# Moving four weight sums from even to odd channel tiles in the gate and up stage of a two-layer block

## The chip, the core and the metric

The kernel runs on one core of a Trainium2 chip. The metric is the device time of one execution in microseconds (us), given as a median of several runs. The engines are PE (matrix products), DVE (elementwise work and PSUM reads), ACT (activations and copies), POOL (elementwise work on SBUF) and SP, which here only issues DMA transfers. Each engine takes its instructions in a fixed order and waits at the first one whose inputs, or whose output buffer, are not ready.

## What is computed

The reference is a mixer block with a mixture of experts, then an attention block, then a feed-forward layer on 1024 tokens of width 1024. Only the last layer matters here:

```
h = rms_norm_2(x, norm_ffn)
gu = h @ w_gate_up                                   # (1024, 1024) @ (1024, 5632)
x = x + (silu(gu[:, :2816]) * gu[:, 2816:]) @ w_down # (1024, 2816) @ (2816, 1024)
```

## The kernel before, in words

`phase6` computes this layer. Both products are done as 2x2 block products with seven multiplications in place of eight (products 1 to 7), each in full precision from a high and a low part of every operand, so that one product is 4 x 3 = 12 matmuls of 128x128 by 512.

**Gate and up.** The 2816 hidden channels make 22 tiles of 128 (`FF`), j = 0 to 21. `seq` lists the products: tiles 0 and 1 mixed, then tile by tile in the order 1, 4, 6, 7, 5, 2, 3 for j = 2 to 19, then 20 and 21 mixed. The main loop (from L2258 on) does four things at step i. It calls `prep(i + 5)`, which turns the weights of the product five steps ahead into a high part on ACT (L1942) and a low part on DVE (L1943). It calls `product(i)` on PE (L1958). It calls `evac(i - 1)`, which reads the finished product from PSUM (DVE L1978 to L1997, ACT L1974, L1994 and L1998) and, where all is there, multiplies gate by up on POOL (`act0` L2001, `act1` L2004). At some steps it adds side work on POOL. The loop is written out by hand for PE, DVE, ACT and POOL: each of these runs the instructions in the order of the code. SP's order is chosen by the scheduler when the program is built.

**Side work.** `load(j)` fetches the weights of a tile, and `sums(j)` forms four sums of them on POOL (L1926 to L1929) for products 5, 6, 7 and 3, just before the first `prep` of tile j. When an odd tile's last product has been read, at the first step of the next even tile, `pair_sums` forms four sums of the activations of the last two tiles on DVE (L2037 to L2040), in buffers called l12 and l34, and `keep` (L2032) stores them to DRAM (`fd`) for the down projection. `right_load(i)` and `right_sums(i)` fetch two blocks of the down projection's weights, form four sums of them on POOL (L2058 to L2061), in buffers r12 and r34, and store them to DRAM (`td`). There are 11 such i. Before the change i = 1 to 9 go to the even tiles 2 to 18, i = 0 to tile 9 and i = 10 to tile 15.

**Buffers.** All of these live in slots of 4 KB per partition, taken from the front of a queue (`get`) and given back at its end (`put`). `put` is a matter of the order of the code only; the engine that first writes the new tenant waits until the last reader of the old one, a store to DRAM too, is done. So a different order of `get` and `put` gives every later buffer another slot, and other waits.

**Down projection.** After the loop the same scheme runs over the stored activations and sums. It reads `fd`, `td` and the weights back.

The mark of a tile that is used below is the start of `act1` (L2004) on POOL, once a tile, or the DVE instruction that leads to it (L1997).

Of the kernel before, what the change touches and what calls it, by code (L numbers as in the profile page):

```python
# [49 lines left out]
class _K:  # L50
# [1819 lines left out]
    FF = 22  # L1870
# [3 lines left out]
    def phase6(self):  # L1874
        nc, I = self.nc, self.I
        V, G, A = nc.vector, nc.gpsimd, nc.scalar
        FF, H = self.FF, 512
# [4 lines left out]
        FP = FF // 2  # L1882
# [10 lines left out]
        def get(key, shape=(P, 1024), dt=F32):  # L1893
            held[key] = free.popleft()
            return self.S(held[key], shape, dt)

        def put(*keys):
            for k in keys:
                free.append(held.pop(k))
# [18 lines left out]
        def load(j):  # L1918
            for n, c in (("g", 0), ("u", FF)):
                st[j][n] = get((n, j), (P, KC, P))  # L1920
                nc.sync.dma_start(st[j][n], w[:, :, (c + j) * P:(c + j + 1) * P])
# [13 lines left out]
        def prep(i):  # L1935
            prepped.append(i)
            j, p = seq[i]
            if "done" not in st[j]:
                sums(j)
            src = st[j][self.PAIRS[p][0]]  # L1940
            t = get(("w", i), (P, 2, 4, P), F32R)
            A.activation(t[:, 0], src, AF.Copy)  # L1942
            V.tensor_sub(t[:, 1], src, t[:, 0])  # L1943
            st[j]["w", p] = t
            d = st[j]["done"]
            d.add(p)
            for k, n in (("g", {1, 2}), ("u", {4}), ("s12", {5, 6}), ("s34", {7, 3})):
                if n <= d and p in n:
                    put((k, j))

        def product(i):
            j, p = seq[i]
            tag, ps = st[j]["b", p] = bank()
            t = st[j].pop(("w", p))
            xs = X[self.PAIRS[p][1]]
            for k in range(4):
                for n, (a, b) in enumerate(((0, 0), (0, 1), (1, 0))):
                    nc.tensor.matmul(ps, t[:, a, k], xs[k][:, b], start=(k == 0 and n == 0), stop=(k == 3 and n == 2))  # L1958
            put(("w", i))
# [70 lines left out]
        def keep(i, o, src, dst=fd):  # L2030
            n = src.shape[-1]
            nc.sync.dma_start(dst[i * P:(i + 1) * P, o * H:o * H + n], src)  # L2032
# [17 lines left out]
        def right_load(i):  # L2050
            for n in range(2):
                right[i, n] = get(("r", i, n))
                nc.sync.dma_start(right[i, n], wd[:, 2 * i + n, :])

        def right_sums(i):
            a, b = right.pop((i, 0)), right.pop((i, 1))
            t12, t34 = get(("r12", i), (P, 2, H)), get(("r34", i), (P, 2, H))
            G.tensor_sub(t12[:, 0], a[:, H:], a[:, 0:H])  # L2058
            G.tensor_sub(t12[:, 1], b[:, H:], t12[:, 0])
            G.tensor_sub(t34[:, 0], b[:, H:], a[:, H:])  # L2060
            G.tensor_sub(t34[:, 1], b[:, 0:H], t12[:, 1])  # L2061
            keep(i, 0, t12.rearrange("p a b -> p (a b)"), td)
            keep(i, 2, t34.rearrange("p a b -> p (a b)"), td)
            put(*((n, i) for n in ("r12", "r34")), *(("r", i, n) for n in range(2)))
# [103 lines left out]
        def pump(now, spare, most=2, splits=1):  # L2168
            n = 0
            while (coming and coming[0][0] + LAG <= now and need[coming[0][1][:2]] <= now + AHEAD  # L2170
                   and n < splits and len(free) > spare):
                op_split()
                n += 1
            n = 0
            while ops and n < most and (loads[0] % 2 or (len(free) > spare + KEEP and len(raw) < RAWS)):
                op_load(now)
                n += 1
# [6 lines left out]
        def x_load():  # L2184
            for t in xs[:2]:
                x[t] = get(("x", t))
                nc.sync.dma_start(x[t], self.h2d[t * P:(t + 1) * P, :])
            del xs[:2]

        with self.tc.manual_schedule(engines={E.PE, E.DVE, E.Activation, E.Pool}):  # L2190
# [67 lines left out]
            for i in range(6, len(seq)):  # L2258
                j = seq[min(i + LEAD + 7, len(seq) - 1)][0]
                if "g" not in st[j]:  # L2260
                    load(j)
                while i + LEAD >= len(prepped) and len(prepped) < len(seq):
                    prep(len(prepped))
                product(i)
                evac(i - 1)
                j, p = seq[i]
                if 2 <= j < FF - 2 and (j % 2 == 0 or j in (9, 15)):
                    m = j // 2 if j % 2 == 0 else {9: 0, 15: FP - 1}[j]
                    if p == 1:
                        right_load(m)  # L2270
                    if p == 4:
                        right_sums(m)
                if i + 1 == len(seq) or seq[i][0] == FF - 1:
                    put(*((self.PAIRS[p][1], k) for k in range(4)))
                if i >= len(seq) - 14:
                    if i >= len(seq) - XL:
                        x_load()
                    pump(4 * (i - len(seq)), 6 if i < len(seq) - 8 else 12 - SP * (8 - len(xs)), 4, 4)
# [123 lines left out]
```

## Time and profile before

| what | value |
|---|---|
| time, median of 3 runs | 2239.24 us (2236.61 to 2244.52) |
| time of the profiled execution | 2236.43 us |
| its span, first to last instruction | 2234.6 us |
| what lies around the span | 1.8 us |
| PE busy over the span | 91% |
| DVE, ACT, POOL busy over the span | 67%, 40%, 40% |
| gate and up, the tiles that go one by one (j = 2 to 19) | 1573 to 1942 us |

A row of the timeline gives the start of a group of instructions, its length, engine, line of the program, operation and operands, how many instructions it merges, and in brackets how long the engine had been idle before it and what ended that. A row of the chain of waits gives start, length and what was being waited for.

### The profile page before, as it was taken

To read this page: it belongs to the slowest core of one execution; us is meant where nothing else is said; L and a number is where in the kernel's file an instruction comes from. 1 tells how busy PE (TensorE), PEld (TensorE's weight loads), DVE (VectorE), ACT (ScalarE), POOL (GpSimd) and SP (SyncE) were. 2 spreads that over 40 slices of the span, in tenths; PEclk is the share of its full clock that TensorE was granted. 3 is DMA by queue.
4 is the path that set the end of the run, shared out by engine and by line. 5 is a ranking of instruction groups with operands and counts; after the bars stand their busy time and mean duration, and the time that the engine had idled before them with its cause. 6 is when DMAs were issued, how large, how long until landed. Compare 5 with 4: busy or idle time off the path is not lost.

```text
span 2234.6 us, 30292 instructions
## 1 busy us (share of the span) xinstructions
PE 2031.7 (91%) x10594; PEld 1499.3 (67%) x10594; DVE 1496.2 (67%) x2264; ACT 901.4 (40%) x1589; POOL 902.2 (40%) x655
## 2 busy tenths in 40 slices
PE   4988999998899998999868998999999899989995
PEld 2677888887455654666527874687878787767774
DVE  6687886526454534767426349637877777699998
ACT  2544447412244423645305149534222222244443
POOL 2365352331111121222112027305656666567786
PEclk9999999899699999999979999999999999999998
DMA  7352110416799899999984310321454454575541
GB/s 266 123 187 78 38 29 29 134 41 245 294 384 350 310 332 392 355 385 373 381 319 145 119 38 2 133 95 55 153 170 156 163 171 148 184 264 167 193 151 76
DMA packets 204739, 426.09 MB, mean 191 GB/s; under 512 B 18580, under 2 KB 99202, under 8 KB 204578
## 3 DMA queue, kind: packets, MB, share of 16 engines
q1 hardware_dynamic: 195218, 402.62, 49.9%
q0 software_dynamic: 9360, 21.46, 4.1%
q8 instruction: 85, 1.39, 0.3%
q14 instruction: 76, 0.62, 0.1%
HBM read 361.36 MB, written 65.01 MB: 191 GB/s over the span
## 4 chain that ended last, share of the span: by engine, by line
PE 41%; DMA 21%; DVE 18%; issue 10%; POOL 5%; ACT 3%; SPq 1%; POOLq 0%; DVEq 0%; ACTq 0%
DMA s<-w 9%; PE a L282 7%; PE a L270 4%; PE a L812 4%; DMA x2d<-s,dstp 3%; DVE s L1943 2%; PE t L2326 2%; PE a L2326 2%; DMA s<-w_ada 2%; DMA s<-ffn_w_gate_up 2%; DMA x2d<-s,dsti 2%; PE a L1412 2%; DVE s L2161 2%; DVE s L509 1%; PE r L2326 1%
## 5 line engine op out<-in xcount | busy, mean ns | idle before, releaser
L1344 DVE TENSOR_TENSOR s<-s,s 128x1024 fp32r<-128x1024 f32 x168 | 206.2, 1240 | 122.1 <-ACT s L1343 117.3
L282 PE MATMUL a<-s,s 128*128 128x512 f32 x1008 | 244.6, 400 | 9.9 <-ACT s L503 9.9
L1343 ACT ACTIVATE s<-s 128x1024 fp32r<-128x1024 f32 x168 | 175.8, 1057 | 152.8 <-PE t L1403 74.5
L282 PEld LDWEIGHTS a<-s,s 128*128 128x128 f32 x1008 | 190.4, 191 | 52.3 <-ACT s L503 10.2
L1943 DVE TENSOR_TENSOR s<-s,s 128x512 fp32r<-128x512 f32 x154 | 162.9, 1074 | 73.6 <-ACT s L1942 73.6
L1958 PE MATMUL a<-s,s 128*128 128x512 f32 x708 | 173.5, 395 | 1.2 <-ACT s L1942 1.0
L1958 PE MATMUL t<-s,s 128*128 128x512 f32 x648 | 161.4, 404 | 13.1 <-DVE s L1943 9.6
L1354 POOL DMA_INDIRECT s<-h2d,toki x38 | 42.9, 1129 | 312.1 <-PE r L1370 148.7
L1958 PEld LDWEIGHTS a<-s,s 128*128 128x128 f32 x708 | 133.6, 189 | 33.5 <-ACT s L1942 1.9
L1942 ACT ACTIVATE s<-s 128x512 fp32r<-128x512 f32 x154 | 91.1, 622 | 159.6 <-DVE s L1943 71.7
L1958 PEld LDWEIGHTS t<-s,s 128*128 128x128 f32 x648 | 124.4, 193 | 44.9 <-DVE s L1943 11.3
L2161 DVE TENSOR_TENSOR s<-s,s 128x512 fp32r<-128x512 f32 x129 | 139.0, 1114 | 0.0
L1403 PE MATMUL t<-s,s 128*128 128x512 f32 x384 | 119.5, 407 | 5.3 <-DVE s L1487 3.1
L1958 PE MATMUL r<-s,s 128*128 128x512 f32 x492 | 120.2, 394 | 0.3
L1403 PE MATMUL a<-s,s 128*128 128x512 f32 x336 | 106.5, 413 | 7.0 <-DVE s L1372 3.5
L270 PE MATMUL a<-s,s 128*128 128x512 f32 x432 | 107.1, 399 | 2.7 <-DVE s L1602 2.7
L1958 PEld LDWEIGHTS r<-s,s 128*128 128x128 f32 x492 | 92.2, 188 | 22.3 <-DVE s L1943 1.1
L2160 ACT ACTIVATE s<-s 128x512 fp32r<-128x512 f32 x154 | 84.7, 621 | 41.4 <-POOL s L2161 18.1
L2326 PE MATMUL a<-s,s 128*128 128x512 f32 x348 | 94.7, 396 | 4.6 <-DVE s L2347 1.7
L2326 PE MATMUL t<-s,s 128*128 128x512 f32 x348 | 90.8, 399 | 8.0 <-DVE hraw L2338 2.5
L1412 PE MATMUL a<-s,s 128*32 128x256 f32 (+1 forms) x736 | 89.5, 464 | 8.1 <-ACT s L1386 3.3
L812 PE MATMUL a<-s,s 128*128 128x512 f32 x384 | 92.7, 397 | 0.6 <-DVE s L666 0.6
(576 smaller groups left out, 4374.3 us busy)
## 6 DMA issues: line engine op xcount, KB each, us to landing
s<-w SPq DMA_DIRECT2D x384, 512.0 KB
s<-w_ada SPq DMA_DIRECT2D x48, 512.0 KB
s<-ffn_w_gate_up SPq DMA_DIRECT2D x44, 512.0 KB
s<-fd SPq DMA_DIRECT2D x77, 256.0 KB
fd<-s SPq DMA_DIRECT2D x33, 512.0 KB
h2d<-s SPq DMA_DIRECT2D x24, 512.0 KB
s<-w_in SPq DMA_DIRECT2D x22, 512.0 KB
s<-ffn_w_down SPq DMA_DIRECT2D x22, 512.0 KB
```

Of the source, the lines that this page charges most:

```text
L270: nc.tensor.matmul(ps[:m], a[:, k, :], b(k, h), start=(k == 0 and n == 0), stop=(k == KC - 1 and n == 2))
L282: nc.tensor.matmul(ps[h][:m], a[:, k, :], b(k, h), start=(k == 0 and n == 0), stop=(k == KC - 1 and n == 2))
L812: nc.tensor.matmul(ps, a.of(k, t), W[k][:, b], start=(k == 0 and n == 0), stop=(k == 7 and n == 2))
L1343: nc.scalar.activation(hi, raw, AF.Copy)
L1344: V.tensor_sub(lo, raw, hi)
L1403: nc.tensor.matmul(pp[h], a[:, k // 4, s], w[:, h * 512:(h + 1) * 512], start=(k == 0 and n == 0), stop=(k == 7 and n == 2))
L1412: nc.tensor.matmul(p_[M * g:M * g + M, 0:N], x[:, k_, :], w[:, :, g, :], start=(k_ == 0), stop=(k_ == 7))
L1942: A.activation(t[:, 0], src, AF.Copy)
L1943: V.tensor_sub(t[:, 1], src, t[:, 0])
L1958: nc.tensor.matmul(ps, t[:, a, k], xs[k][:, b], start=(k == 0 and n == 0), stop=(k == 3 and n == 2))
L2161: (G if loads[1] % SHARE == SHARE - 1 else V).tensor_sub(u[:, 1], t, u[:, 0])
L2326: nc.tensor.matmul(ps[p], a[:, e, q * P:(q + 1) * P], b[:, f], start=(i == g[0] and n == 0), stop=(i == g[-1] and n == 2))
```

## The change

Nothing is added or taken away: the same 11 loads, 44 sums and 22 stores are called at other steps. The sums i = 1 to 9 go from tile 2i to tile 2i + 1, at the same two steps of the tile (load with product 1, sums with product 4). The sums i = 0 and i = 10 go from tiles 9 and 15 to tiles 8 and 14, and there to later steps: load with product 7, sums with product 2.

```diff
-                if 2 <= j < FF - 2 and (j % 2 == 0 or j in (9, 15)):
-                    m = j // 2 if j % 2 == 0 else {9: 0, 15: FP - 1}[j]
+
+                if 2 < j < FF - 2 and j % 2:
                     if p == 1:
-                        right_load(m)
+                        right_load(j // 2)
                     if p == 4:
-                        right_sums(m)
+                        right_sums(j // 2)
+                if j in (8, 14):
+                    if p == 7:
+                        right_load({8: 0, 14: FP - 1}[j])
+                    if p == 2:
+                        right_sums({8: 0, 14: FP - 1}[j])
```

In the rows below a buffer is written as slot and number: s8_18032 is the tenant 18032 of slot 8. POOL from `act1` of tile 9 to `act1` of tile 10, and up to the sums after it, before:

```order
L2004 TENSOR_TENSOR s8_17937<-s8_17937,hraw_17918 128x512
L2058 TENSOR_TENSOR s44_18026<-s7_18004 128x512
L2059 TENSOR_TENSOR s44_18026<-s13_18006,s44_18026 128x512
L2060 TENSOR_TENSOR s34_18027<-s13_18006,s7_18004 128x512
L2061 TENSOR_TENSOR s34_18027<-s13_18006,s44_18026 128x512
L1926 TENSOR_TENSOR s8_18038<-s23_17878 128x512
L1927 TENSOR_TENSOR s8_18038<-s8_18038,s43_17876 128x512
L1928 TENSOR_TENSOR s5_18039<-s43_17876,s23_17878 128x512
L1929 TENSOR_TENSOR s5_18039<-s43_17876,s8_18038 128x512
L2001 TENSOR_TENSOR s34_18095<-s34_18095,m_18024 128x512
L2004 TENSOR_TENSOR s34_18095<-s34_18095,hraw_18076 128x512
L1926 TENSOR_TENSOR s20_18176<-s16_18036 128x512
```

The same place now:

```order
L2004 TENSOR_TENSOR s29_17937<-s29_17937,hraw_17918 128x512
L1926 TENSOR_TENSOR s13_18026<-s43_17878 128x512
L1927 TENSOR_TENSOR s13_18026<-s13_18026,s16_17876 128x512
L1928 TENSOR_TENSOR s33_18027<-s16_17876,s43_17878 128x512
L1929 TENSOR_TENSOR s33_18027<-s16_17876,s13_18026 128x512
L2001 TENSOR_TENSOR s5_18083<-s5_18083,m_18020 128x512
L2004 TENSOR_TENSOR s5_18083<-s5_18083,hraw_18064 128x512
L2058 TENSOR_TENSOR s22_18164<-s43_18142 128x512
L2059 TENSOR_TENSOR s22_18164<-s6_18144,s22_18164 128x512
L2060 TENSOR_TENSOR s13_18165<-s6_18144,s43_18142 128x512
L2061 TENSOR_TENSOR s13_18165<-s6_18144,s22_18164 128x512
L1926 TENSOR_TENSOR s8_18176<-s31_18024 128x512
```

In the even tile 10 the next tile's four sums now follow `act1` at once, and in the odd tile 11 the four down sums stand between `act1` and the next tile's sums.

SP at the start of tile 10 now stores the activations of tile 9 and then l12 and l34:

```order
L2032 DMA fd_15856<-s29_17937 128x1024
L2032 DMA fd_15856<-s8_17996 128x1024
L2032 DMA fd_15856<-s23_17997 128x1024
L1921 DMA s38_18172<-ffn_w_gate_up_2 128x8x128
L2053 DMA s43_18142<-ffn_w_down_2 128x1024
```

l12 is in slot 8 and l34 in slot 23. ACT in tile 10, from the conversion for product 3 on, before:

```order
L1942 ACTIVATE s31_18008<-s22_17881 128x512
L1974 ACTIVATE m_18024<-r1_17979 128x512
L1942 ACTIVATE s22_18044<-s43_17876 128x512
L1942 ACTIVATE s27_18060<-s23_17878 128x512
L1942 ACTIVATE s44_18078<-s8_18038 128x512
```

and now, there and then at the same place of tile 11:

```order
L1942 ACTIVATE s38_18004<-s27_17881 128x512
L1974 ACTIVATE m_18020<-r1_17979 128x512
L1942 ACTIVATE s8_18032<-s16_17876 128x512
L1942 ACTIVATE s23_18048<-s43_17878 128x512
L1942 ACTIVATE s29_18066<-s13_18026 128x512
...
L1974 ACTIVATE m_18162<-a1_18125 128x512
L1942 ACTIVATE s23_18182<-s20_18022 128x512
L1942 ACTIVATE s22_18198<-s31_18024 128x512
L1942 ACTIVATE s13_18216<-s8_18176 128x512
```

In the even tile the two conversions behind `u1` (L1974) now write the slots of l12 and l34; in the odd tile the second and third write the slots of r12 and r34 (22 and 13), which the POOL rows above fill in the same tile.

## Rows read from the trace of the kernel before

**Rows 1.** The page: span, and busy time of the engines.
```profile
span 2234.6 us, 30292 instructions
```

**Rows 2.** Waits of PE from 1555 to 1960 us: total, times, longest.
```profile
PE t L1958 <- DVE s L1943: 9.6, 3, 5.6
```

**Rows 3.** Timeline of PE: start, length, engine, line, what, count, idle before.
```profile
1744.84 4.63 PE L1958 MATMUL t<-s,s 128*128 128x512 f32 x10 [5.63 <-DVE s L1943]
...
1774.56 2.93 PE L1958 MATMUL r<-s,s 128*128 128x512 f32 x12
...
1813.36 2.94 PE L1958 MATMUL r<-s,s 128*128 128x512 f32 x12
```

**Rows 4.** Timeline of POOL: `act1` of tiles 1, 8 to 11, 14, 15, 17, two sums.
```profile
1573.12 1.29 POOL L2004 TENSOR_TENSOR s<-s,hraw 128x512 f32<-128x512 f32 x1 [0.18 <-ACT hraw L1998]
...
1714.56 1.29 POOL L2004 TENSOR_TENSOR s<-s,hraw 128x512 f32<-128x512 f32 x1 [1.89 <-ACT hraw L1998]
1715.80 1.77 POOL L2058 TENSOR_TENSOR s<-s 128x512 f32<-128x512 f32 x1
...
1726.01 1.29 POOL L1929 TENSOR_TENSOR s<-s,s 128x512 f32<-128x512 f32 x1
...
1736.09 1.30 POOL L2004 TENSOR_TENSOR s<-s,hraw 128x512 f32<-128x512 f32 x1 [1.89 <-ACT hraw L1998]
...
1759.96 1.30 POOL L2004 TENSOR_TENSOR s<-s,hraw 128x512 f32<-128x512 f32 x1 [1.89 <-ACT hraw L1998]
...
1775.16 1.29 POOL L2004 TENSOR_TENSOR s<-s,hraw 128x512 f32<-128x512 f32 x1 [1.89 <-ACT hraw L1998]
...
1838.15 1.30 POOL L2004 TENSOR_TENSOR s<-s,hraw 128x512 f32<-128x512 f32 x1 [1.89 <-ACT hraw L1998]
...
1858.36 1.30 POOL L2004 TENSOR_TENSOR s<-s,hraw 128x512 f32<-128x512 f32 x1 [1.89 <-ACT hraw L1998]
...
1897.14 1.29 POOL L2004 TENSOR_TENSOR s<-s,hraw 128x512 f32<-128x512 f32 x1 [1.89 <-ACT hraw L1998]
```

**Rows 5.** Timeline of DVE: the even tile 12, from L1997 to L1997.
```profile
1773.75 0.67 DVE L1997 TENSOR_TENSOR hraw<-hraw,t 128x512 f32<-128x512 f32 x1
1776.49 1.76 DVE L2037 TENSOR_TENSOR s<-s,s 128x512 f32<-128x512 f32 x1 [2.07 <-POOL s L2004]
...
1781.59 1.80 DVE L2040 TENSOR_TENSOR s<-s,s 128x512 f32<-128x512 f32 x1
1783.31 0.68 DVE L1943 TENSOR_TENSOR s<-s,s 128x512 fp32r<-128x512 f32 x1
...
1797.30 0.68 DVE L1997 TENSOR_TENSOR hraw<-hraw,t 128x512 f32<-128x512 f32 x1
```

**Rows 6.** Chain of waits: stores of l34 (fd) and of r34 (td).
```profile
1721.84 4.15 DMA td<-s
...
1783.42 3.13 DMA fd<-s
...
1845.37 3.12 DMA td<-s
```

**Rows 7.** Timeline of DVE: the even tile 18, behind a wait for a store.
```profile
1915.16 0.69 DVE L1943 TENSOR_TENSOR s<-s,s 128x512 fp32r<-128x512 f32 x1 [7.45 <-ACT s L1942]
...
1923.89 0.67 DVE L1997 TENSOR_TENSOR hraw<-hraw,t 128x512 f32<-128x512 f32 x1
```

**Rows 8.** Timeline of ACT: the odd tile 15, which has down sums before the change.
```profile
1845.54 0.63 ACT L1942 ACTIVATE s<-s 128x512 fp32r<-128x512 f32 x1 [5.94 <-DMA td<-s]
1848.63 0.63 ACT L1942 ACTIVATE s<-s 128x512 fp32r<-128x512 f32 x1 [2.46 <-DMA td<-s]
```

**Rows 9.** Timeline of DVE: the pair sums after tile 19, with POOL idle.
```profile
1939.95 0.68 DVE L1997 TENSOR_TENSOR hraw<-hraw,a 128x512 f32<-128x512 f32 x1
1942.71 0.69 DVE L2037 TENSOR_TENSOR s<-s,s 128x512 f32<-128x512 f32 x1 [2.08 <-POOL s L2004]
...
1944.64 0.68 DVE L2040 TENSOR_TENSOR s<-s,s 128x512 f32<-128x512 f32 x1
```

## The prediction

> **What bounds the kernel now.** I read PE's waits first, then the timelines of the four engines in the gate and up stage, then the chain of waits. The profiled execution took 2236.43 us, 1.8 more than its span [rows 1]; it is 2.8 under the median of 2239.24. PE goes through 14 products, two tiles, in 1813.36 - 1774.56 = 38.8 us, so 19.4 a tile, when nothing stops it [rows 3]. In tiles 2 to 19 it is stopped only a few times, nearly always by the conversion of weights on DVE (9.6 us in three waits, the longest 5.6) [rows 2], and after the long one it is slow for a while: ten matmuls take 4.63 us where twelve take 2.93 [rows 3].
>
> Behind PE runs a chain of its own: ACT, DVE and POOL in fixed orders, five products of preparation ahead. Its length per tile is read from mark to mark. A plain odd tile takes 1775.16 - 1759.96 = 15.2 us [rows 4]. An even tile with pair sums on DVE and down sums on POOL takes 1797.30 - 1773.75 = 23.55 [rows 5]. Together 38.75: as much as PE needs for the pair. The odd tiles that also carry down sums take more: tile 9 takes 1736.09 - 1714.56 = 21.5, tile 15 takes 1858.36 - 1838.15 = 20.2 [rows 4]. PE's long wait, 5.63 us at 1744.84 [rows 3], follows tile 9. The 16 tiles 2 to 17 take the chain 1897.14 - 1573.12 = 324.0 us [rows 4], where PE alone would take 16 x 19.4 = 310.4. So the stage is balanced, and where the chain needs more than 38.8 a pair PE has to wait, since its lead is used up.
>
> **The odd tile after the change.** Tiles 3, 5, ... 17 get what tiles 9 and 15 had: the down sums between `act1` and the next tile's sums, at the same steps, and the order shows the same slots: the second and third conversion behind `u1` write the slots of r12 and r34, which must first be summed and stored. In tile 15 these conversions waited 5.94 and 2.46 us for the two stores [rows 8]; DVE and all that reads the products stood behind them. I take the mean of tiles 9 and 15, 20.9 us, in place of 15.2, with 20.2 and 21.5 as bounds. The stores differ: the second took 4.15 us in tile 9 and 3.12 in tile 15 [rows 6].
>
> **The even tile after the change.** No row shows this one, so I put it together from L1997 of tile 12, time 0 [rows 5]. `act1` starts at 1775.16 - 1773.75 = 1.41 [rows 4, 5] and frees the pair sums at 2.74. POOL now goes on to the next tile's sums at once, so the pair sums run beside four POOL instructions as before (there beside the down sums), and end at 1781.59 + 1.80 - 1773.75 = 9.64 [rows 5]. The conversions behind `u1` now write the slots of l12 and l34. l12 is ready two sums earlier and its store is over in time. The store of l34 can only start at the end of the pair sums: issued 1783.42, 3.13 us long, it is over at 12.80 [rows 5, 6]. ACT then needs 0.63 for the conversion [rows 8], and DVE starts its part at about 13.5. From such a start, behind a wait for a store and with the later conversions ready, tile 18 needed 1923.89 - 1915.16 = 8.73 to L1997 [rows 7]. That makes 22.2 us. What it saves against 23.55: three conversions on DVE are no longer slowed by POOL, and the store of r34 no longer holds the activation buffer. What it pays is the wait for l34. Bounds: the even tile of before, 23.55, from above; from below 15.8. This is the plain odd tile's 15.2 with its three conversions at 0.68 in place of about 1.6 each, plus four pair sums at the 0.69 that they take with POOL idle (2.6 us [rows 9]) plus 0.85 more wait for `act1`. I take 22.2, since the pair sums do meet POOL and the slot of l34 is in the order; it is nearest to 23.55.
>
> The page "SBUF — State Buffer" of the Trainium skill (section "Who interferes with whom") says that a DVE instruction with two SBUF inputs and a POOL instruction that reads SBUF shut each other out for the whole instruction. The rows show 6.8 us for the four pair sums beside POOL against 0.69 each alone [rows 5, 9], so they do disturb each other. Taken strictly, four times 1.29 + 0.69 would be 7.9, 1.1 us more an even tile, and the eight even tiles would add some 9 us to the sum below. The measured 6.8 is what I use.
>
> **The extra sums.** For i = 0 and 10 the sums move to the end of tiles 8 and 14. Their loads need the slots of the activations that the pair sums read, so they start late; the sums then run beside three or so DVE conversions, and the next tile's load of down weights sits in the slots of r12 and r34 of these sums, behind their stores. I put 5 us on each. This is an estimate from the extra in tiles 9 and 15 before, 21.5 - 15.2 = 6.3 and 20.2 - 15.2 = 5.0 [rows 4]; bounds 0 and 6.3.
>
> **The end of the stage.** Tile 18 took 1923.89 + 1.41 - 1897.14 = 28.2 us before [rows 4, 7], 7.45 of it on the store of r34. Now the conversion that waited has an activation slot that is free after the pair sums, at about 10.8, and 8.73 later the tile is over: 19.5, a gain of 8.7. Tile 19 took 1939.95 - 1923.89 = 16.1 [rows 7, 9]. It gets the sums of i = 9 ahead of the eight sums of tiles 20 and 21: conversions wait for slots of the down weights until about 9, so some 17.4 (+1.3). POOL has `act1`, 12 sums and two products: eight sums took 1726.01 + 1.29 - 1715.80 = 11.5 [rows 4], so `act1` of tile 19 ends at about 2.7 + 17.3 + 2.6 = 22.6, 5.2 after L1997 in place of 2.76 [rows 9]; with some contention I put +3 on the last pair sums, which DVE must pass before the last conversions. Together -8.7 + 1.3 + 3 = -4.4. The down projection reads the same data in the same order, and what comes late at its start stays late.
>
> **The sum.** Tiles 2 to 17: 8 x (22.2 + 20.9) + 2 x 5 = 354.8 against 324.0, +30.8. With the end, +26.4. PE's work lies inside it: 310.4 and its slow matmuls still fit. 2236.4 + 26.4 = 2262.8, so 2263 in the terms of the profiled execution; 2.8 more against the median, inside the range.
>
> **The rivals.**
> - *The even tile gains more than the odd one loses.* If the pair sums and the sums on POOL hardly met, or l34 were stored earlier, the even tile would come toward 15.8. It decides at 18.0: with 20.9 that is 38.9 a pair. Below it PE sets the pace, the waits after tiles 9 and 15 go, and 13.6 (324.0 - 310.4) and 4.4 are gained: 2218. For it: POOL has half its work in that place. Against it: the store starts only behind the last pair sum [rows 5, 6]. Chance 6%.
> - *About no change.* The even tile at 20 and the odd at the lower 20.2, the extra sums hidden: 8 x 40.2 = 321.6, less 4.4 at the end: 2230 to 2243. It needs two of my terms at or under their lower end. Chance 7%.
> - *The down weights come late.* SP's order now puts the first load of these weights behind a gate load that waits for a product on PE, and the second ahead of the activation's store. When PE itself waits, these slip, and POOL waits for weights in the odd tile before it gets to the sums. Three to six us on eight odd tiles: 24 to 48 more, 2287 to 2311. For it: SP's queue already stood on DVE and POOL before. Against it: by the times above the load is issued at about 15 and needed at 25. Chance 9%.
>
> That the change does not do what it says is excluded by the order.
>
> **How the numbers follow.** Forecast 78%: slower, 2263. Low end: even 21.5, odd 20.2, extras 2 each: 337.6, +13.6 - 4.4, so 2246. High end: even 23, odd 21.5, extras 6.3: 368.6, +44.6 and no gain at the end: 2281. To hold the time 8 times in 10 the range must reach a little into the neighbours: down to 2243, the slower edge of no change, and up to 2288, the lower edge of the late weights. It leaves out the gain, half of no change and most of the late weights. Slower by over 0.3% (6.7 us, about what a measurement of this kernel can tell from none): 87%, the forecast and the late weights; within 0.3% 7%; faster 6%.
>
> **What would show it.** Marks on POOL 20 to 21.5 us apart in odd tiles and about 22 in even ones, where they were 15.2 and 23.6. ACT waiting for fd stores in each even tile and for td stores in each odd one. PE waiting 2 to 4 us for L1943 once a pair, from tile 4 on, right behind the pair sums, and matmuls at half pace after it. Tile 18 under 21 us. It is wrong if even tiles take less than 19, or if POOL is found waiting for down weights in odd tiles.

## The result, and the profile after

The changed kernel takes 2260.6 us (2258.7 to 2264.3) against 2237.9 for the kernel before: slower by a ratio of 1.010, 95% interval 1.0077 to 1.0124. The forecast was 2263, slower; the time is 2.4 us under it. The sum was worked out from the profiled execution, though, so its effect is the fairer measure: 26.4 us more were forecast, 22.7 came by the medians. The profiled execution took 2258.72 us, 22.3 more than that of before.

```profile
span 2256.9 us, 30284 instructions
```

The windows of tiles 2 to 17, from `act1` of tile 1 to `act1` of tile 17, give length, then the busy time and the number of instructions of PE, of PE's weight loads, DVE, ACT and POOL, and at the end the granted clock, the busy share of the DMA engines and the GB/s that they moved. First the kernel before, then the changed one:

```profile
1573.12:1897.14 324.02, 314.17 (x1336) 253.80 (x1335) 244.72 (x256) 90.89 (x161) 208.83 (x137) 0.98 0.49 163
```

```profile
1576.38:1923.68 347.30, 323.23 (x1350) 259.40 (x1350) 230.67 (x256) 90.76 (x161) 195.10 (x137) 0.97 0.45 152
```

The 16 tiles take 23.3 us more. PE's idle time in them rose from 324.02 - 314.17 = 9.85 to 347.30 - 323.23 = 24.07, 14.2 of the 23.3. A matmul took 239 ns on average in place of 235, with a granted clock of 0.97 in place of 0.98 as the mean of the stretch: 1344 matmuls (16 tiles of 84) by 4.2 ns are another 5.7. The remaining 3.3 are 14 more records in the window. Waits of PE from 1555 to 1985 us (total, times, longest), which answer to [rows 2]:

```profile
PE t L1958 <- DVE s L1943: 17.7, 5, 5.6
PE r L1958 <- DVE s L1943: 5.3, 3, 2.9
PE a L1958 <- ACT s L1942: 2.6, 2, 1.8
```

POOL's timeline gives the new pair of tiles, as [rows 4] gave the old one. Tile 12 runs from the first of these rows to the second, tile 13 from the second to the last:

```profile
1792.22 1.30 POOL L2004 TENSOR_TENSOR s<-s,hraw 128x512 f32<-128x512 f32 x1 [1.89 <-ACT hraw L1998]
...
1813.91 1.30 POOL L2004 TENSOR_TENSOR s<-s,hraw 128x512 f32<-128x512 f32 x1 [1.89 <-ACT hraw L1998]
1815.17 1.76 POOL L2058 TENSOR_TENSOR s<-s 128x512 f32<-128x512 f32 x1
...
1822.49 1.65 POOL L1927 TENSOR_TENSOR s<-s,s 128x512 f32<-128x512 f32 x1
...
1834.20 1.30 POOL L2004 TENSOR_TENSOR s<-s,hraw 128x512 f32<-128x512 f32 x1 [1.89 <-ACT hraw L1998]
```

The even tile takes 21.7, the odd one 20.3: 42.0 us a pair where PE needs 38.8. ACT shows what each waits for. The first two rows are the even tile 12, the last two the odd tile 13:

```profile
1801.75 0.63 ACT L1942 ACTIVATE s<-s 128x512 fp32r<-128x512 f32 x1 [8.61 <-DVE s L1943]
1803.11 2.19 ACT L1942 ACTIVATE s<-s 128x512 fp32r<-128x512 f32 x4 [0.72 <-DMA fd<-s]
...
1821.33 0.64 ACT L1942 ACTIVATE s<-s 128x512 fp32r<-128x512 f32 x1 [5.97 <-DMA td<-s]
1824.17 0.63 ACT L1942 ACTIVATE s<-s 128x512 fp32r<-128x512 f32 x1 [2.21 <-POOL s L1927]
```

In the even tile it is the store of l34 (fd). In the odd tile the first wait is the store of r12 (td), as forecast. The second, which is the last before the tile runs on, names POOL's sum L1927 and not the store of r34. That is so in the six plain odd tiles; in tiles 9 and 15, which stand behind the extra sums, both waits are for td. ACT's waits over the stage (total, times, longest):

```profile
ACT s L1942 <- DMA td<-s: 56.7, 10, 7.8
ACT s L1942 <- DVE s L2040: 50.9, 7, 7.3
ACT s L1942 <- DMA fd<-s: 34.6, 10, 10.0
ACT s L1942 <- POOL s L1927: 15.1, 7, 2.4
```

### The profile page after: what moved, and what is told of

Its sections match the earlier page's. It is cut to its first block, busy times and chain, and to the rows that moved or that the text cites. A ratio compares the mean times of both kernels' runs of the same rounds, so it can differ in the third digit from the quotient of the medians.

```text
span 2256.9 us, 30284 instructions
## 1 busy us (share of the span) xinstructions
PE 2039.4 (90%) x10594; PEld 1505.3 (67%) x10594; DVE 1480.2 (66%) x2264; ACT 901.1 (40%) x1589; POOL 885.4 (39%) x655
## 4 chain that ended last, share of the span: by engine, by line
PE 48%; DVE 20%; DMA 13%; issue 9%; POOL 6%; ACT 3%; SPq 1%; DVEq 0%; POOLq 0%; ACTq 0%
PE a L282 7%; PE a L270 4%; PE a L812 4%; PE t L1403 3%; DMA x2d<-s,dstp 3%; PE a L1412 3%; DMA s<-w 2%; DVE s L2161 2%; PE a L1403 2%; DMA s<-w_ada 2%; DVE s L509 2%; PE t L1412 2%; DMA x2d<-s,dsti 2%; PE a L1455 2%; DMA fd<-s 2%
## 5 line engine op out<-in xcount | busy, mean ns | idle before, releaser
L282 PE MATMUL a<-s,s 128*128 128x512 f32 x1008 | 245.5, 402 | 10.8 <-ACT s L503 10.8
L1943 DVE TENSOR_TENSOR s<-s,s 128x512 fp32r<-128x512 f32 x154 | 148.1, 971 | 119.8 <-ACT s L1942 119.1
L282 PEld LDWEIGHTS a<-s,s 128*128 128x128 f32 x1008 | 191.1, 192 | 53.4 <-ACT s L503 11.1
L1958 PE MATMUL t<-s,s 128*128 128x512 f32 x648 | 162.5, 406 | 20.5 <-DVE s L1943 17.7
L1958 PE MATMUL a<-s,s 128*128 128x512 f32 x708 | 175.2, 398 | 3.0 <-ACT s L1942 2.6
L1958 PEld LDWEIGHTS t<-s,s 128*128 128x128 f32 x648 | 124.7, 194 | 53.3 <-DVE s L1943 20.4
L1958 PEld LDWEIGHTS a<-s,s 128*128 128x128 f32 x708 | 134.7, 191 | 36.1 <-ACT s L1942 3.9
L2161 DVE TENSOR_TENSOR s<-s,s 128x512 fp32r<-128x512 f32 x129 | 139.3, 1116 | 0.0
L1403 PE MATMUL a<-s,s 128*128 128x512 f32 x336 | 105.2, 408 | 7.0 <-DVE s L1372 3.5
L270 PE MATMUL a<-s,s 128*128 128x512 f32 x432 | 108.7, 403 | 2.6 <-DVE s L1602 2.6
L2160 ACT ACTIVATE s<-s 128x512 fp32r<-128x512 f32 x154 | 84.7, 621 | 41.6 <-POOL s L2161 18.2
L2331 PE MATMUL a<-s,s 128*128 128x512 f32 x348 | 95.1, 398 | 3.8 <-DVE s L2352 1.6
L270 PEld LDWEIGHTS a<-s,s 128*128 128x128 f32 x432 | 80.9, 191 | 19.3 <-DVE s L1602 2.9
```

Source lines behind the costliest of these rows:

```text
L270: nc.tensor.matmul(ps[:m], a[:, k, :], b(k, h), start=(k == 0 and n == 0), stop=(k == KC - 1 and n == 2))
L282: nc.tensor.matmul(ps[h][:m], a[:, k, :], b(k, h), start=(k == 0 and n == 0), stop=(k == KC - 1 and n == 2))
L1403: nc.tensor.matmul(pp[h], a[:, k // 4, s], w[:, h * 512:(h + 1) * 512], start=(k == 0 and n == 0), stop=(k == 7 and n == 2))
L2161: (G if loads[1] % SHARE == SHARE - 1 else V).tensor_sub(u[:, 1], t, u[:, 0])
L2331: nc.tensor.matmul(ps[p], a[:, e, q * P:(q + 1) * P], b[:, f], start=(i == g[0] and n == 0), stop=(i == g[-1] and n == 2))
```

## The experiments

The table gives the starts of `act1` on POOL in each kernel's profile, as differences. "Even" and "odd" are means over tiles 2, 4, 6, 10, 12, 16 and 3, 5, 7, 11, 13, 17. Ratios are to the kernel before, with their 95% intervals. Between two kernels that both differ from it by a few us, the tiles of the profiles tell more than the medians. "Raw slots" are those of the two loaded blocks of down weights, "activation slots" those of the two activations that the pair sums read, "extras" the sums i = 0 and 10; "first" means given back ahead of the slots that still have to be stored.

| kernel | even | odd | 8 + 9 | 14 + 15 | 2 to 17 | 18 | 19 | time us | ratio |
|---|---|---|---|---|---|---|---|---|---|
| before | 23.9 | 15.2 | 45.2 | 44.5 | 324.0 | 28.2 | 16.1 | 2237.9 | 1 |
| after | 21.6 | 20.2 | 48.6 | 47.7 | 347.3 | 19.6 | 20.8 | 2260.6 | 1.0100 (1.0077 to 1.0124) |
| E1 after, raw slots first | 21.6 | 20.4 | 45.1 | 43.9 | 340.7 | 19.7 | 21.4 | 2253.2 | 1.0072 (1.0046 to 1.0098) |
| E2 after, activation slots first | 19.7 | 20.3 | 43.0 | 43.3 | 326.0 | 23.3 | 20.7 | 2233.1 | 0.9976 (0.9959 to 0.9994) |
| E3 both | 19.7 | 20.3 | 43.1 | 43.1 | 326.3 | 23.4 | 21.0 | 2233.1 | 0.9977 (0.9961 to 0.9993) |
| E4 before, raw slots first | 22.2 | 15.2 | 42.5 | 42.8 | 309.7 | 26.2 | 16.0 | 2221.5 | 0.9914 (0.9886 to 0.9941) |
| E5 after, one sum more | 21.6 | 21.6 | 47.8 | 48.2 | 355.4 | 19.6 | 20.8 | 2264.7 | 1.0111 (1.0090 to 1.0132) |
| E6 after, down sums late | 22.0 | 17.4 | 42.2 | 42.4 | 321.0 | 19.7 | 26.8 | 2236.1 | 0.9999 (0.9985 to 1.0012) |
| E7 E6 and E2 | 19.9 | 18.2 | 38.1 | 39.7 | 306.3 | 23.3 | 27.6 | 2220.3 | 0.9916 (0.9896 to 0.9936) |
| E8 before, extras alone | 23.6 | 15.2 | 40.1 | 40.9 | 314.1 | 26.9 | 16.0 | 2227.8 | 0.9961 (0.9946 to 0.9976) |
| E9 after, sums early | 23.5 | 19.7 | 52.2 | 52.7 | 363.8 | 21.5 | 18.7 | 2275.0 | 1.0156 (1.0130 to 1.0183) |
| E10 E9 and E1 | 23.2 | 17.7 | 48.8 | 48.9 | 342.8 | 21.5 | 21.6 | 2254.4 | 1.0067 (1.0042 to 1.0092) |
| E11 E4 and E8 | 22.3 | 15.2 | 42.6 | 40.3 | 307.9 | 26.1 | 16.1 | 2218.1 | 0.9904 (0.9879 to 0.9929) |

**E1: the odd tile without its store waits.**

```diff
-            put(*((n, i) for n in ("r12", "r34")), *(("r", i, n) for n in range(2)))
+            put(*(("r", i, n) for n in range(2)), *((n, i) for n in ("r12", "r34")))
```

> The changed kernel, with one line of right_sums turned round: the slots of the two loaded blocks of down weights are given back ahead of those of r12 and r34. The second and third conversion behind u1 in an odd tile then write slots that only POOL's sums have read, and r12 and r34 come to the activation and to the conversion after it. If the stores of r12 and r34 make the odd tile long (the prediction's step), the ACT waits for td of 6 us and more go, the odd tile falls from 20.2 to about 18 us, and the time falls by 8 x 2.2, to about 2243 (2235 to 2251). If POOL's order does it (four down sums ahead of the next tile's four), the odd tile stays at 20 us and the time at 2260.

The plain odd tile did not move (20.4). ACT's timeline of E1 in the odd tile 13, which begins with the `act1` at 1808.96:

```profile
1814.95 0.64 ACT L1942 ACTIVATE s<-s 128x512 fp32r<-128x512 f32 x1 [4.53 <-POOL s L2060]
1819.30 0.64 ACT L1942 ACTIVATE s<-s 128x512 fp32r<-128x512 f32 x1 [3.72 <-POOL s L1927]
```

The wait for td is gone, the first conversion starts 1.4 us earlier, and the next one starts 10.3 us after `act1` as it did in the changed kernel, since the sum it reads is not there. The time, 2253.2, lies between what the two causes would have given: the 6.6 us that tiles 2 to 17 gained lie in the pairs with the extra sums (3.5 and 3.8).

**E2 and E3: the even tile without its store wait.** `pair_sums` gives nothing back, and `out` gives all four slots:

```diff
-                    put(("act", j), ("act", j - 1))
+                    put(("act", j), ("act", j - 1), ("l12", i), ("l34", i))
...
-            else:
-                put(("l12", i), ("l34", i))
```

> The changed kernel, with the slots of the two activations given back ahead of those of l12 and l34. In an even tile the two conversions behind u1 then wait for the end of the pair sums and no longer for the store of l34; l34 comes to the activation. If that store sets the even tile, it falls from 21.6 by some 2.9 us to 18.7, and the time by 8 x 2.9, to about 2237 (2230 to 2248). If the pair sums themselves, slowed by POOL, set it, the even tile stays at 21 us and more, and the time at 2255 to 2261.

> Both turned orders in the changed kernel. If the two store waits are all that the change added, even and odd tile together come to about 18.7 + 18 = 36.7 us, under the 38.8 that PE needs, so PE sets the pace: tiles 2 to 17 fall from 347.3 to some 311 to 316, the time to about 2224 to 2232, below the kernel before. If the POOL order or the pair sums hold it, it stays over 2245.

The even tile fell from 21.6 to 19.7. ACT of E2 in tile 12, which begins at 1779.94, starts right behind the last pair sum:

```profile
1788.22 2.72 ACT L1942 ACTIVATE s<-s 128x512 fp32r<-128x512 f32 x5 [7.35 <-DVE s L2040]
```

That is 8.3 us after the mark; in the changed kernel the second conversion came at 10.9. So the store of l34 is what held the even tile, 1.9 us of it. E2 frees the first conversion from the store of l12 as well, but in the changed kernel that conversion started clearly behind the last pair sum in tile 12 only (ACT's wait there is 8.6 us, in the other plain even tiles 7.2 to 7.4). The tile was expected at 18.7; that it stops at 19.7 was not followed up. The median fell by 27 us, below the kernel before. E3 is E2 again: the expected fall of the odd tile to 18 did not come, for the reason seen in E1.

**E5: one POOL instruction more in the odd tile.**

```diff
-            G.tensor_add(s12[:, 0], u[:, 0:4], u[:, 4:8])
+            for _ in range(2 if j % 2 == 0 and 2 < j < FF - 2 else 1):
+                G.tensor_add(s12[:, 0], u[:, 0:4], u[:, 4:8])
```

> The changed kernel, with the first sum of the gate and up weights of the even tiles 4 to 18 formed twice (L1926 again, into the same place). It adds one POOL instruction of 1.3 to 1.8 us in each of the eight odd tiles, behind the four down sums, their slots and stores unchanged. The theory after the first runs: what sets the odd tile is POOL's order, as the conversion for product 6 waits for L1927 behind act1, four down sums and L1926. Then each odd tile grows by that instruction, 20.2 to about 21.6, and the time by 8 x 1.4, to about 2272 (2268 to 2276). If the stores of r12 and r34 set it (the prediction's step), L1927 comes later beside a wait that is there anyway, and the time stays at 2258 to 2264.

The odd tile grew from 20.2 to 21.6 as POOL's order would have it. The wait for td is 5.96 as it was, and only the wait for the sum grew. ACT's timeline of E5, tile 13, whose lines stand one lower (L1928 is the old L1927):

```profile
1825.43 0.63 ACT L1943 ACTIVATE s<-s 128x512 fp32r<-128x512 f32 x1 [5.96 <-DMA td<-s]
1829.66 0.63 ACT L1943 ACTIVATE s<-s 128x512 fp32r<-128x512 f32 x1 [3.59 <-POOL s L1928]
```

Tiles 2 to 17 grew by 8.1 us, less than the 11 expected: the pairs with the extra sums together did not grow (47.8 and 48.2 against 48.6 and 47.7). The median, 2264.7, is under the 2268 to 2276 expected and nearly in the range of the other cause; it is 4.1 over that of the changed kernel, and the intervals of the two overlap, so the tiles carry this verdict, not the medians.

**E6 and E7: the down sums in POOL's idle time.**

```diff
-                    if p == 4:
+                    if p == 2:
                         right_sums(j // 2)
```

> The changed kernel, with the down sums of the odd tiles formed with product 2 in place of product 4: POOL then does the next tile's four sums first, and the down sums in the time in which it idles ahead of act0. If POOL's order sets the odd tile, it falls from 20.2 to between 15.2 and 17 us; with the even tile at 21.6 the pair is under the 38.8 of PE, PE sets the pace, tiles 2 to 17 fall from 347 to about 311, and the time to about 2225 (2219 to 2235). If the down sums cost the odd tile their price wherever in it they stand, by the loads, by the stores or by holding DVE up, it stays at 19 or more, and the time over 2245.

> The last kernel with the slots of the two activations also given back ahead of those of l12 and l34. With both causes gone an even and an odd tile need 19.7 + 15.2 to 17 = 35 to 37 us, so PE sets the pace with room: 2218 to 2230, within 5 us of the last kernel. Should the last one stay over 2245, this one would be some 16 us under it, the even tiles' part.

The odd tile fell to 17.4. The pair, 22.0 + 17.4 = 39.4, is still over PE's 38.8, and tile 19 became 6 us longer, so E6 stops at 2236 where 2225 was expected. E7, with the even tile short as well, lets PE set the pace: 306.3 us and 2220.3, which is 16 us under E6 where at most 5 were expected. PE is busy for all of E7's 306.3 us; they are fewer than 310.4 because its window, which starts and ends with a mark on POOL, holds 1328 matmuls in place of 1344.

**E9 and E10: POOL's order without the stores, then neither.** The next even tile's sums are formed in the even tile before; r12, r34 and their successors keep their places in the queue of slots.

```diff
+                if 2 <= j < FF - 3 and j % 2 == 0 and p == 2:
+                    sums(j + 2)
```

> The changed kernel, with the four gate and up sums of the even tiles 4 to 18 formed some four products earlier, with product 2 of the even tile before, where POOL idles ahead of act0. The slots and stores of r12 and r34, and who takes their slots, are as in the changed kernel. So in an odd tile the order of POOL can't hold the conversion for product 6 any more; the stores still can. If there are two ends that lie within half a microsecond of each other (L1927 ready 10.2 us after act1, the store of r34 over at some 10.4), the odd tile stays at 19.5 to 20.5 and ACT waits twice for td. If POOL's order is the only cause, the odd tile falls to 17.5 or less. Either way the four sums beside DVE's work in the even tile may cost that tile 0 to 1.5 us. Time: 2254 to 2272 by the first, 2225 to 2242 by the second.

> The last kernel with the slots of the loaded blocks also given back ahead of those of r12 and r34 (the line of the first experiment): POOL's order and the stores are both gone from the odd tile. The two conversions behind u1 then wait for the third and the fourth down sum only, some 6.0 and 7.3 us after act1 in place of 7.4 and 10.2. By the theory of two ends the odd tile falls from 20.2 to about 17.3, where each remedy alone left it at 20; with the even tile at 21.6 to 23 the pair comes to 39 to 40.3, so 2230 to 2245. If the odd tile stays at 20 here too, something that neither run touched sets it.

With the stores alone the odd tile is 19.7, with POOL's order alone 20.4 (E1), with both 20.2, with neither 17.7. ACT's timeline of E9 in the odd tile 11, which begins with the `act1` at 1785.04, and then of E10 in its tile 11, which ends with `act1` at 1787.49:

```profile
1792.48 0.63 ACT L1942 ACTIVATE s<-s 128x512 fp32r<-128x512 f32 x1 [5.99 <-DMA td<-s]
1794.96 1.68 ACT L1942 ACTIVATE s<-s 128x512 fp32r<-128x512 f32 x3 [1.85 <-DMA td<-s]
```

```profile
1775.84 0.63 ACT L1942 ACTIVATE s<-s 128x512 fp32r<-128x512 f32 x1 [4.56 <-POOL s L2060]
1777.11 0.63 ACT L1942 ACTIVATE s<-s 128x512 fp32r<-128x512 f32 x1 [0.65 <-POOL s L2061]
```

In E9 the second conversion comes 9.9 us after the mark and waits for the store of r34; in the changed kernel it came 10.3 after it and waited for L1927. So two ends lie 0.3 us apart. Taking away the store alone gains nothing, POOL's order alone 0.5 us, both 2.5. The times, 2275.0 and 2254.4, are above what was expected, since eight sums now stand one behind the other in the even tile (23.5 and 23.2), and the pairs with the extra sums grew to between 48.8 and 52.7.

**E8, E4 and E11: parts alone, and the shortest kernel.** E8 is the kernel before with the five lines for tiles 8 and 14 and without tiles 9 and 15; E4 is the kernel before with E1's line; E11 has both.

> The kernel before with only the second part of the change: the sums i = 0 and 10 at the end of tiles 8 and 14, those of i = 1 to 9 left in the even tiles. The prediction put 5 us on each at the new place, against 6.3 and 5.0 at the old one: tiles 9 and 15 fall to 15.2, tiles 8 and 14 (and the tile after) rise by about as much, and the time stays at 2234 to 2240. If the new place costs only what the runs with the activations first show (2 to 3 us over two tiles), tiles 2 to 17 fall by 5 to 7 us, to 2231 to 2234. The changed kernel itself showed 6.8 and 5.8 there: by that, 2239.

> The kernel before, with the slots of the loaded blocks given back ahead of those of r12 and r34, and nothing else. Tiles 9 and 15 lose most of their waits for td (21.5 and 20.2 to about 18), the even tile's activation no longer stands on the store of r34 (23.55 to 22 or 23), tile 18 gives back some of its 7.45 us wait. If stores into reused slots are the cost in the kernel before too: 2237.9 less 6 to 15, 2223 to 2232. If not: 2236 to 2240.

> The kernel before with the two edits that shortened it: the slots of the loaded blocks given back first, and the two extra sums in tiles 8 and 14. Each alone brought it to 2221.5 and 2227.8. If PE sets the pace of tiles 2 to 17 with the first edit alone (309.7 us there, 310.4 at 19.4 a tile), the second can add little: 2215 to 2222. If the gains add up, 16 and 9 us: 2212.

The move of the two extra sums alone is a gain of 9 us, more than any of the three cases expected: tiles 8 and 9 fall from 45.2 to 40.1, 14 and 15 from 44.5 to 40.9. There the extra sums cost 1.3 and 2.1 us over a plain pair; in the changed kernel 6.7 and 5.8. POOL's timelines show a part of the difference, first the changed kernel in tiles 8 and 9, then E8 in tile 8:

```profile
1716.12 1.30 POOL L2058 TENSOR_TENSOR s<-s 128x512 f32<-128x512 f32 x1 [6.65 <-DMA s<-ffn_w_down]
...
1732.46 1.30 POOL L2059 TENSOR_TENSOR s<-s,s 128x512 f32<-128x512 f32 x1 [2.18 <-DMA s<-ffn_w_down]
```

```profile
1709.59 1.29 POOL L2058 TENSOR_TENSOR s<-s 128x512 f32<-128x512 f32 x1 [1.37 <-DMA s<-ffn_w_down]
1712.57 1.29 POOL L2059 TENSOR_TENSOR s<-s,s 128x512 f32<-128x512 f32 x1 [1.68 <-DMA s<-ffn_w_down]
```

The wait of 2.18 us is for the odd tile's own load, and no such load stands behind the extra sums in E8. The wait of 6.65 us says less: E8's extra sums come 16.5 us after the mark, later than the changed kernel's 14.3, but cost less there. By the changed kernel's marks the 6.7 us are 3.8 in tile 8 and 2.9 in tile 9. The 2.9 go with E1 (tile 9 falls from 23.1 to 20.3), so there the order of the slots of r12 and r34 is the cause. In tile 8 the store of l34 took longer than in the plain tiles (ACT waits 3.64 us for it in place of some 2.0), and two conversions on DVE that meet the extra sums on POOL take 1.78 and 1.73 us where they take 0.68 in tile 12. Together these come to about 3.8; this part is read from the trace and was not tested.

E4 gains 16 us, a little more than expected: the even tile is 1.7 us shorter, its activation no longer standing on the store of r34. In the kernel before DVE waits for that store in each of the eight even tiles 2 to 16, 14.1 us in all, and in E4 in none. DVE's timeline of the kernel before in tile 12:

```profile
1791.10 0.69 DVE L1986 TENSOR_TENSOR s<-x,a 128x512 f32<-128x512 f32 x1 [1.40 <-DMA td<-s]
```

Tiles 9 and 15 stay at 20.4, where 18 was expected: E1's finding again. In E4 and E11 PE is busy for nearly all of tiles 2 to 17 (309.1 of 309.7 and 307.9 of 307.9), so there was little left for the second edit to gain. E11's 2218.1 is the shortest time of the study, 1% under the kernel before, and within the range expected if the gains don't add; its interval overlaps those of E4 and E7. All that PE waits for in E11 from 1555 to 1960 us:

```profile
PE a L1958 <- ACT s L1942: 0.9, 1, 0.9
```

## Why the prediction was right, and where it was not

**The mechanism.** A chain on ACT, DVE and POOL that needs more than 38.8 us a pair makes PE wait: this held. The pair needs 41.8, PE waits, and E2 is a test of the same model from the other side: the rival "about no change" asked for an even tile at 20 and an odd one at 20.2 and gave 2230 to 2243. E2 has 19.7 and 20.3, and 2233.

**The even tile**, 22.2 forecast, 21.6 measured, cause shown by E2. The step put the conversion behind the store of l34 and the store at 3.13 us. The chain of waits of the changed kernel has one of 2.57 in tile 10, so this term was too large by 0.6; the longest is in tile 8. What comes behind it was right: 8.73 us from DVE's start to L1997 forecast, 1812.49 - 1803.78 = 8.71 in tile 12. The two stores in the chain:

```profile
1710.05 4.19 DMA fd<-s
...
1758.54 2.57 DMA fd<-s
```

The four pair sums in tile 12, beside four sums on POOL, by DVE's timeline:

```profile
1793.55 1.76 DVE L2037 TENSOR_TENSOR s<-s,s 128x512 f32<-128x512 f32 x1 [2.08 <-POOL s L2004]
...
1798.67 1.79 DVE L2040 TENSOR_TENSOR s<-s,s 128x512 f32<-128x512 f32 x1
```

They take 1798.67 + 1.79 - 1793.55 = 6.9 us, as before the change, where [rows 5] give 1781.59 + 1.80 - 1776.49 = 6.9 too; the prediction's 6.8 was a misreading by 0.1. Strict exclusion, as the page "SBUF — State Buffer" of the Trainium skill states it (section "Who interferes with whom"), would make it 7.9 by the estimate in the prediction; the measurement again decides against it, and for the end of the pair sums that the forecast used.

**The odd tile**, 20.9 forecast, 20.2 measured: the size right, the cause only half right. The step read [rows 8] as the cause: two waits for td, so the stores of r12 and r34. It took the mean of tiles 9 and 15; tile 9 carried a longer store, 4.15 us [rows 6]. What it did not ask is what would come next if those stores were gone. POOL's order, which puts L1927 10.2 us behind the mark, ends within 0.3 us of the store of r34, and in the changed kernel it is the later of the two. The number was safe because tiles 9 and 15 held both causes; a forecast for E1 by the same step was wrong. The trace of the kernel before could have told it. In tile 15 the store of r34 was over at 1845.37 + 3.12 = 1848.49 [rows 6], and POOL's timeline there has L1927 ending at 1848.29, 0.2 us earlier:

```profile
1846.67 1.62 POOL L1927 TENSOR_TENSOR s<-s,s 128x512 f32<-128x512 f32 x1
```

**The extra sums**, 5 us each forecast, 6.7 and 5.8 measured. The mechanism stood in the text: late loads, and the next tile's load in the slots of r12 and r34. What was wrong was to price the new place by the old one, which made the move nearly neutral: it gains 9 us in the kernel before (E8). In the changed kernel the order of the slots of r12 and r34 is 3.5 and 3.8 us of the price (E1). What E1 leaves, 3.1 and 1.9 us, was read in tile 8 only, as a longer store of l34 and slower conversions beside the sums, and not tested.

**The sum over tiles 2 to 17**, 354.8 forecast, 347.3 measured: 8 x (0.6 + 0.7) too much on the plain tiles, 2.5 too little on the extra sums.

**The end of the stage.** Tile 18 fell by 8.5 (forecast 8.7). DVE's timeline of the end, which answers to [rows 9]:

```profile
1941.90 0.67 DVE L1997 TENSOR_TENSOR hraw<-hraw,t 128x512 f32<-128x512 f32 x1
...
1961.62 0.67 DVE L1997 TENSOR_TENSOR hraw<-hraw,a 128x512 f32<-128x512 f32 x1
1965.40 0.69 DVE L2037 TENSOR_TENSOR s<-s,s 128x512 f32<-128x512 f32 x1 [3.11 <-POOL s L2004]
...
1967.34 0.68 DVE L2040 TENSOR_TENSOR s<-s,s 128x512 f32<-128x512 f32 x1
```

Tile 19 takes 19.7 us from L1997 to L1997, +3.7 where +1.3 was forecast; the pair sums behind it end 6.4 us after L1997 in place of 5.4, +1.0 where +3 was forecast. The sum, +4.7 against +4.3, is right, its parts are not: twelve sums on POOL held the tile itself.

**The whole.** From `act1` of tile 1 to the last pair sum the changed kernel takes 19.4 us more (26.4 forecast). Another 3.3 of the 22.3 lie ahead of that mark, at 1576.38 in place of 1573.12. In the profiles of the eleven other kernels here it stands anywhere from 1571.5 to 1581.3, so that part is not put down to the change; it brought the time nearer to the forecast than its terms were, which is luck.

**The other rivals.** The even tile did not come to 18. The down weights are late only at the two extra sums and in the tiles after them (POOL waits for them four times, 16.7 us in all, in tiles 8, 9, 14 and 15), not in the plain odd tiles. **The marks named in advance** came: odd tiles 20 to 21.5 apart, even about 22, ACT waiting ten times each for td and fd, tile 18 under 21. PE's waits come right behind the pair sums in every even tile from tile 4 to 18 but tile 12, and are 1.0 to 5.6 us long rather than 2 to 4; two more, of 1.8 and 1.1 us, stand in the odd tiles 9 and 15. The slower matmuls behind them were named, their size was not.

## What to carry to other kernels

When a wait is read as the cause, ask what the waiting instruction would wait for next: here a store and a sum on another engine ended 0.3 us apart, so either remedy alone gained 0.5 us a tile or nothing, and both together 2.5. In a queue of buffers the order of giving back is a free parameter: the buffers whose last reader is an engine go back ahead of those that still have to be stored; one line of that kind gained 16 us in the kernel before (E4), where the best move of the work gained 9 (E8), and another gained 27 in the changed kernel (E2), where the best move gained some 24 (E6). Only what the engines wait for last pays: in the plain odd tiles such a line gained nothing (E1). Parts of a change are measured apart: the part that looked neutral gained 9 us alone, and the two together lost 23.

## What the runs showed of the hardware

In the chain of waits of the changed kernel, stores of 512 KB from one buffer took between 2.56 and 4.19 us in the same stage; what a buffer waits is not one number. With PE's waits come slower matmuls: some 5.7 us on top of 14.2 us of waiting, at a mean granted clock of 0.97 in place of 0.98. Eight POOL instructions in a row behind `act1` (E9) made the even tile 1.9 us longer although POOL still idled ahead of `act0`; how much of that is DVE slowed by POOL and how much the later stores was not told apart.
